# Key roots on ScalarE, the first latent block ahead of the third pair's output, and within-chunk products ahead of the values, in a two-block transformer kernel

## The chip, the cores and the metric

One core of one Trainium2 chip runs the whole program once. The metric is the device time of that execution in microseconds; lower is better.

## What is computed

Two transformer blocks over 512 tokens of width 1024, all in float32. The second block's mixer holds what the change touches: a gated delta rule in chunks (8 heads of width 128, forwards and backwards) beside a latent attention.

```python
qkv = silu(centred_conv(qkv, conv_w))          # 5 taps along the tokens
q, k = l2norm(q), l2norm(k)                    # x * rsqrt(sum(x*x) + 1e-6)
beta = sigmoid(beta_logit); g = -exp(a_log) * softplus(decay_logit + dt_bias)
# per chunk, gc = cumsum(g):
a_mat  = strict_lower((k*beta) @ k.T * exp(gc_i - gc_j))
t_mat  = inverse(eye + a_mat)
u, w   = t_mat @ (v*beta), t_mat @ (k*beta*exp(gc))
qk     = lower(q @ k.T * exp(gc_i - gc_j))
# scan over chunks with state s (128 x 128):
v_new  = u - w @ s
o      = (q*exp(gc)) @ s + qk @ v_new
s      = s*exp(gc_last) + (k*exp(gc_last - gc)).T @ v_new
o_gdn  = rms(o, w_norm) * silu(z)
```

Beside it the latent attention takes 704 columns of the same projection of 512 tokens and 256 context tokens (384 query latents, 256 key and value latents, 64 rotary), normalizes them and goes on from there; 2048 further columns give the gates of the two branches.

## The kernel before

Every large product is made in three products of rounded parts (high by high, high by low, low by high: lines 234, 235 and 237 in `mm3s`). A weight block of 256 columns comes by DMA in two groups of 128 x 1024 values (`weights`). ScalarE makes the high half (line 178) and VectorE the low half (line 179). Raw, high and low tiles share six buffers of one tag. The k, v and q blocks of all pairs are an exception: their halves were made earlier in the program, lie in DRAM as `parts` and come in ready by DMA (line 164). The z, latent and gate blocks are split when they are used.

The gated delta stage (`gdn`) goes over four pairs of heads. Per pair p:

- `inputs`: products for k (512 tokens and 256 context tokens per head), then q (512 tokens). Results land in one of two `pg` banks of PSUM. `conv` copies a result twice on ScalarE, once as it is (line 1254) and once scaled by the middle tap (line 1255), both from PSUM; VectorE adds the four other taps (line 1261), ScalarE applies Silu (line 1263). k is turned by TensorE (line 1291), its squares are summed on ScalarE (line 1316). The sums go to GpSimd, which adds 1e-6 (line 1319), takes the power -1/2 (line 1321) and multiplies to the root (line 1322).
- `values`: products for v like those for k; when v is turned, line 1296 scales it by k's root.
- `betas`: logarithm (line 1351) and reciprocal (line 1353) of the sums, put into the per-token factors `nb` and `bd`.
- `within`: k by k and k by q products (lines 1375, 1377), decays as exponentials on ScalarE (lines 1384 to 1387), masked products on VectorE (lines 1389 to 1391) and the diagonal blocks copied into `X` (lines 1395 and 1397).
- `states`: the inverse of all 32x32 diagonal blocks on VectorE (lines 1405 to 1419, a chain of 62 steps on one engine), block products that complete the inverse (lines 1425 to 1473), and the scan of six steps (lines 1477 to 1542).
- `output`: z products, Silu (line 1550), norm, turn (line 1565) and product with z (line 1567).

The text puts `states(p)` first, then for p+1 `inputs`, `values`, `betas`, `within`, and then `output(p)`. After the last `states` stands `tail()`: the latent products (`mla_latent`, three blocks of 256, 256 and 192 columns, copied to six pages `Z` on line 987) and four blocks of gates (line 863); then the last output.

What sets the order: the SP queue, which issues the loads, keeps the order of the text (`tc.manual_schedule(engines={SP})`). The other engines' instructions are put in an order when the program is built, earlier text first among those that can go; on the chip each engine runs its own list in order. So a later step can fill an engine's gap, but an instruction that waits holds up everything behind it on its engine. Pages of 3 KB (14 of them) hold convolutions, keys, values and `Z`.

Of the kernel before, what the change touches and what calls it, by code (L numbers as in the profile page):

```python
# [75 lines left out]
class Kernel:  # L76
# [766 lines left out]
    def second(self):  # L843
        nc, ap = self.nc, self.ap
# [14 lines left out]
        def gates(j, fs, take, s="a", W=None):  # L859
            for f in fs:  # L860
                for i, ps in self.proj_feat(H, w, 4832 + 1024 * j + f * 256, W=W if f == fs[0] else None):
                    p = self.page([512], s=s)
                    nc.scalar.activation(p, ps, AF.Sigmoid)
                    take(2 * f + i, p)

        def away(j):
            return lambda i, p: nc.scalar.dma_start(GD[j, i], p)

        def tail():
            self.latent = self.mla_latent(H, HC, w)  # L870
            gates(0, range(4), away(0))

        OD = self.gdn(H, HC, w, tail)
        self.wlo_eng = nc.vector
        self.psum(**BANKS_C)
        self.phase(**PHASE_C)
# [92 lines left out]

    def mla_latent(self, H, HC, w):  # L970

        nc, ap = self.nc, self.ap
        act, dve = nc.scalar.activation, nc.vector
        con = self.hb
# [7 lines left out]
        for f0, fn in ((0, 256), (256, 256), (512, 192)):  # L982
            W = self.weights(w, 0, 8, 4128 + f0, fn)
            for X, n, o in ((H, 4, 2), (HC, 2, 0)):
                for t2, ps in self.proj_tok(X, None, 0, n, fn, W):
                    for i in range(2):
                        act(Z[o + 2 * t2 + i][:, f0:f0 + fn], ps[:, i], AF.Copy)
        kr = con.tile([128, 6, 64], F32, name="kr")
        ssr = con.tile([128, 6], F32, name="ssr")
        CQ = [con.tile([128, 2, 512], F32R, name="cq", tag=f"inv{k}") for k in range(3)]  # L990
# [28 lines left out]
        for i in range(2):  # L1019
            nc.scalar.dma_start(gq[64 * i:64 * i + 64], bass.AP(tensor=nm.tensor, offset=nm.offset + 128, ap=[[1, 64], [1, 1]]))  # L1020
        nc.gpsimd.tensor_scalar(ropq, ropq, gq, None, op0=OP.mult)
        return [[c[:, 0], c[:, 1]] for c in CQ], CKV, kr, ssr, ropq, gq

    def mla(self, first, CQ, CKV, kr, ssr, ropq, gqr):

# [210 lines left out]
        g["rows"] = rg  # L1236
        yield g

    def gdn(self, H, HC, w, tail):
        nc, ap = self.nc, self.ap  # L1240
        mm, act, dve = nc.tensor.matmul, nc.scalar.activation, nc.vector
        con = self.const
# [2 lines left out]
        tm = [con.tile([128, 136], F32, name=f"invt{v}") for v in range(2)]  # L1245
        nc.gpsimd.memset(X, 0.0)

        def conv(ps, tile):

            raw, acc = (self.page([sum(p.shape[1] for p in ps)]) for _ in range(2))  # L1250
            o = 0
            for p in reversed(ps):
                n = p.shape[1]
                act(raw[:, o:o + n], p, AF.Copy)
                act(acc[:, o:o + n], p, AF.Copy, scale=cw[:, 48 + tile:49 + tile])  # L1255
                for i in (0, 1, 3, 4):
# [43 lines left out]
        def inputs(pair):  # L1300


            h0 = 2 * pair
            qT, sq_, kT, ktok = ([] for _ in range(4))
            fk = fv = None
            if pair == 0:
                fv = None, ahead(2048)[1]
                fk = ahead(1024)
            kc = [conv(ps, 8 + h0 + f) for f, ps in enumerate(feat(1024 + pair * 256, True, fk))]
            n2, root = [], []  # L1310
            for f, (c, raw) in enumerate(kc):
                kt = self.page([6, 128])
                turn(c, kt)
                ss = self.tmp.tile([128, 6], F32, name="kss")
                for t in range(6):
                    act(raw[:, t * 128:t * 128 + 128], kt[:, t], AF.Square, accum_out=ss[:, t:t + 1])
                n2.append(self.hb.tile([128, 6], F32, name=f"kn2{f}", bufs=2))
                root.append(self.hb.tile([128, 6], F32, name=f"krt{f}", bufs=2))
                nc.gpsimd.tensor_scalar(n2[f], ss, 1e-6, None, op0=OP.add)
                r = self.hb.tile([128, 6], F32, name="krs", bufs=2)  # L1320
                nc.gpsimd.tensor_tensor(r, n2[f], self.mhalf[:, :6], op=OP.pow)
                nc.gpsimd.tensor_tensor(root[f], r, n2[f], op=OP.mult)
                kT.append(c.rearrange("p (a b) -> p a b", a=6))
                ktok.append(kt)
            qc = [conv(ps, h0 + f) for f, ps in enumerate(feat(pair * 256, False))]
            for q, sq in qc:
                qT.append(q)
                act(sq, q, AF.Square)
                pq = self.bank([128, 4], "pt")
                for t in range(4):  # L1330
                    mm(pq[:, t:t + 1], sq[:, t * 128:t * 128 + 128], ones, start=True, stop=True)
                s1 = self.tmp.tile([128, 4], F32, name="qss")
                dve.tensor_copy(s1, pq)
                sq_.append(self.rstd(s1, 1.0 / 128, 128e-6, "qrs"))
            return (qT, kT, ktok), (root, sq_), n2, fv

        def values(pair, root, fv):

            vtok = []
            for f, ps in enumerate(feat(2048 + pair * 256, True, fv)):  # L1340
                c, _ = conv(ps, 16 + 2 * pair + f)
                vt = self.page([6, 128])
                turn(c, vt, root[f])
                vtok.append(vt)
            return vtok

        def betas(pair, n2):
            h0, nb, bd = 2 * pair, [], []
            for f in range(2):
                ln = self.hb.tile([128, 6], F32, name="kln", bufs=2)  # L1350
                act(ln, n2[f], AF.Ln)
                inv = self.hb.tile([128, 6], F32, name="kin", bufs=2)
                dve.reciprocal(inv, n2[f])
                for out, nm, v, op in ((nb, "nb", ln, OP.subtract), (bd, "bd", inv, OP.mult)):
                    out.append(self.hb.tile([128, 6, 2], F32, name=f"k{nm}{f}", bufs=2))
                    dve.tensor_tensor(out[f], g[nm][:, :, h0 + f::8], v[:, :, None].to_broadcast([128, 6, 2]), op=op)
            return nb, bd

        D2 = range(2)
# [219 lines left out]
        for pair in range(4):  # L1579
            O = states(pair, *keys, vtok, bd, *EM)  # L1580
            sq_ = rest[1]
            if pair < 3:
                keys, rest, n2, fv = inputs(pair + 1)
                vtok = values(pair + 1, rest[0], fv)
                nb, bd = betas(pair + 1, n2)
                EM = within(pair + 1, *keys[:2], nb)
            else:
                tail()
            output(pair, O, sq_)
        return OD  # L1590

# [52 lines left out]
```

## Time and profile before

| what | value |
|---|---|
| median of 3 runs | 2276.74 us (2273.09 to 2277.0) |
| the profiled execution | 2269.84 us, span 2268.0 us |
| PE (TensorE) busy | 2166.3 us, 96% |
| DVE (VectorE) busy | 1186.8 us, 52% |
| ACT (ScalarE) busy | 1019.6 us, 45% |
| POOL (GpSimd) busy | 257.4 us, 11% |
| mean granted TensorE clock | 0.986 |

PE is the matrix engine and PEld its weight loads. A row in order of time gives start and duration in microseconds, engine, line, operation, output and inputs by the program's names, shape and count; square brackets hold the idle time of that engine before it and what ended it. The granted clock is 1.00 at 2.4 GHz and 0.50 at 1.2 GHz.

### The profile page before, as it was taken

The numbers are of one execution on the slowest core, as the hardware profiler recorded it, in microseconds if no ns is written. First come the engines' busy times: TensorE is split into PE (matmuls) and PEld (weight loads), VectorE is DVE, ScalarE is ACT, GpSimd is POOL, SyncE is SP. The second block draws the span as 40 slices with busy tenths as digits, with TensorE's granted clock in tenths as the row PEclk, the third lists the DMA queues.
The fourth block names the chain that finished last, engine by engine and source line by source line (L and its number), as shares of the span: only waits on it lengthen the run. The fifth ranks groups of instructions, "written<-read, shape, count | busy, mean of one in ns | idle before, by whom it ended". The sixth has DMA issues, their size and how long they took to land. (4 is left out here: it accounts for less than half of the span.)

```text
span 2268.0 us, 38197 instructions
## 1 busy us (share of the span) xinstructions
PE 2166.3 (96%) x15367; PEld 1921.6 (85%) x15367; DVE 1186.8 (52%) x2636; ACT 1019.6 (45%) x2072; POOL 257.4 (11%) x411
## 2 busy tenths in 40 slices
PE   7999999999999999988999998999999998999999
PEld 7889988788889889867787888789998797898988
DVE  3654453656443233658687775337775444434343
ACT  4542243545443232666666664446564224314231
POOL 0221000001000001203121211201110011020102
PEclk9999999999999999999999998999999999999999
DMA  5233476555772332521222110331013442323232
GB/s 171 74 132 122 159 262 212 173 189 187 248 254 88 98 107 89 183 75 53 75 67 89 53 61 13 97 116 37 30 38 110 169 140 73 99 90 102 94 93 103
DMA packets 195816, 262.05 MB, mean 116 GB/s; under 512 B 12343, under 2 KB 157495, under 8 KB 195639
## 3 DMA queue, kind: packets, MB, share of 16 engines
q1 hardware_dynamic: 188864, 244.61, 33.3%
q10 hardware_dynamic: 6775, 15.00, 1.8%
q8 instruction: 121, 1.98, 0.3%
q14 instruction: 56, 0.46, 0.1%
HBM read 223.39 MB, written 36.18 MB: 114 GB/s over the span
## 5 line engine op out<-in xcount | busy, mean ns | idle before, releaser
L179 DVE TENSOR_TENSOR wlo<-wraw,whi 128x1024 fp32r<-128x1024 f32 (+2 forms) x267 | 321.7, 1205 | 413.6 <-PE pg L235 204.8
L178 ACT ACTIVATE whi<-wraw 128x1024 fp32r<-128x1024 f32 (+2 forms) x267 | 277.0, 1037 | 445.1 <-DMA wraw<-in_w_mlp_out 104.5
L234 PE MATMUL pg<-xhi,whi 128*128 128x512 f32 (+1 forms) x1104 | 428.8, 391 | 25.3 <-ACT a L1255 15.9
L235 PE MATMUL pg<-xlo,whi 128*128 128x512 f32 (+1 forms) x1104 | 425.0, 387 | 0.0
L237 PE MATMUL pg<-xhi,wlo 128*128 128x512 f32 (+1 forms) x1104 | 293.5, 385 | 2.3 <-DVE wlo L179 2.3
L234 PEld LDWEIGHTS pg<-xhi,whi 128*128 128x128 f32 x1104 | 210.6, 191 | 72.5 <-ACT a L1255 18.1
L235 PEld LDWEIGHTS pg<-xlo,whi 128*128 128x128 f32 x1104 | 210.5, 191 | 37.0
L237 PEld LDWEIGHTS pg<-xhi,wlo 128*128 128x128 f32 x1104 | 202.9, 190 | 41.3 <-DVE wlo L179 3.0
L234 PE MATMUL pg<-whi,xhi 128*128 128x256 f32 (+1 forms) x608 | 160.3, 293 | 3.5 <-ACT whi L178 2.6
L235 PE MATMUL pg<-whi,xlo 128*128 128x256 f32 (+1 forms) x608 | 156.5, 288 | 0.0
L234 PE MATMUL sc<-whi,a 128*128 128x256 f32 x560 | 138.2, 281 | 1.6 <-ACT whi L178 1.6
L234 PE MATMUL pg<-whi,a 128*128 128x256 f32 x560 | 138.1, 281 | 0.5 <-DVE a L148 0.5
L235 PE MATMUL sc<-whi,a 128*128 128x256 f32 x560 | 138.4, 281 | 0.0
L235 PE MATMUL pg<-whi,a 128*128 128x256 f32 x560 | 138.0, 280 | 0.0
L234 PEld LDWEIGHTS pg<-whi,xhi 128*128 128x128 f32 x608 | 118.2, 194 | 10.6 <-ACT whi L178 5.2
L235 PEld LDWEIGHTS pg<-whi,xlo 128*128 128x128 f32 x608 | 117.9, 194 | 0.7 <-issue 0.4
L1261 DVE SCALAR_TENSOR_TENSOR a<-a,convw,a 128x511 f32<-128x511 f32 (+3 forms) x160 | 98.2, 642 | 20.1 <-ACT a L1255 19.2
L234 PEld LDWEIGHTS sc<-whi,a 128*128 128x128 f32 x560 | 105.6, 189 | 2.0 <-ACT whi L178 1.8
L237 PE MATMUL pg<-wlo,xhi 128*128 128x256 f32 (+1 forms) x608 | 101.5, 288 | 5.7 <-DVE wlo L179 5.7
L936 POOL TENSOR_TENSOR a<-a,a 128x256 f32<-128x256 f32 x64 | 48.8, 763 | 511.2 <-DVE a L935 510.5
L234 PEld LDWEIGHTS pg<-whi,a 128*128 128x128 f32 x560 | 105.6, 189 | 0.9 <-DVE a L148 0.9
L235 PEld LDWEIGHTS sc<-whi,a 128*128 128x128 f32 x560 | 106.0, 189 | 0.2
(477 smaller groups left out, 4543.1 us busy)
## 6 DMA issues: line engine op xcount, KB each, us to landing
wraw<-in_w_in SPq DMA_DIRECT2D x56, 512.0 KB
fraw<-in_w_mod SPq DMA_DIRECT2D x48, 512.0 KB
parts<-fraw SPq DMA_DIRECT2D x48, 512.0 KB
wraw<-in_w_gate_up SPq DMA_DIRECT2D x44, 512.0 KB
wraw<-in_w_mlp_in SPq DMA_DIRECT2D x32, 512.0 KB
wraw<-in_w_mlp_out SPq DMA_DIRECT2D x32, 512.0 KB
whi<-parts SPq DMA_DIRECT2D x26, 512.0 KB
wlo<-parts SPq DMA_DIRECT2D x26, 512.0 KB
```

The source lines that it names most:

```text
L178: nc.scalar.activation(hi, raw, AF.Copy)
L179: self.wlo_eng.tensor_tensor(lo, raw, hi.bitcast(F32), op=OP.subtract)
L234: mm(out, A[k][0], B[k][0], start=start and k == 0, stop=False)
L235: mm(out, A[k][late], B[k][1 - late], start=False, stop=False)
L237: mm(out, A[k][1 - late], B[k][late], start=False, stop=stop and k == n - 1)
L936: nc.gpsimd.tensor_tensor(self.x[t][:, cs], self.x[t][:, cs], u, op=OP.add)
L1261: dve.scalar_tensor_tensor(y, v, wi, y, op0=OP.mult, op1=OP.add)
```

## The change

Three things. First, the root of k's norm and its logarithm come from ScalarE: one Ln over both heads' sums with 1e-6 as its bias, and one Exp of half of that; VectorE adds 1e-6 for the reciprocal. GpSimd's three instructions per head are gone. With it, `conv` makes its second, scaled copy from the first copy in SBUF and no longer from PSUM. Second, the tail becomes a generator in two pieces: the first block of latents is issued after the third pair's states and before the third pair's output, the rest after the last states. Third, for pairs 1 to 3 `betas` and `within` stand ahead of `values`; for pair 0 the order stays.

```diff
-        def tail():
-            self.latent = self.mla_latent(H, HC, w)
+        def beside():
+            yield from self.mla_latent(H, HC, w)
             gates(0, range(4), away(0))
+            yield
...
                         act(Z[o + 2 * t2 + i][:, f0:f0 + fn], ps[:, i], AF.Copy)
+            if f0 == 0:
+                yield
...
+        eps = con.tile([128, 1], F32, name="keps")
+        nc.gpsimd.memset(eps, 1e-6)
...
                 act(raw[:, o:o + n], p, AF.Copy)
-                act(acc[:, o:o + n], p, AF.Copy, scale=cw[:, 48 + tile:49 + tile])
+                act(acc[:, o:o + n], raw[:, o:o + n], AF.Copy, scale=cw[:, 48 + tile:49 + tile])
...
-                    act(raw[:, t * 128:t * 128 + 128], kt[:, t], AF.Square, accum_out=ss[:, t:t + 1])
-                n2.append(self.hb.tile([128, 6], F32, name=f"kn2{f}", bufs=2))
-                root.append(self.hb.tile([128, 6], F32, name=f"krt{f}", bufs=2))
-                nc.gpsimd.tensor_scalar(n2[f], ss, 1e-6, None, op0=OP.add)
-                r = self.hb.tile([128, 6], F32, name="krs", bufs=2)
-                nc.gpsimd.tensor_tensor(r, n2[f], self.mhalf[:, :6], op=OP.pow)
-                nc.gpsimd.tensor_tensor(root[f], r, n2[f], op=OP.mult)
+                    act(raw[:, t * 128:t * 128 + 128], kt[:, t], AF.Square, accum_out=ss[:, f, t:t + 1])
...
+            ln = self.hb.tile([128, 2, 6], F32, name="kln", bufs=2)
+            act(ln, ss, AF.Ln, bias=eps)
+            root = self.hb.tile([128, 2, 6], F32, name="krt", bufs=2)
+            act(root, ln, AF.Exp, scale=0.5)
...
+            inv = self.hb.tile([128, 2, 6], F32, name="kin", bufs=2)
+            dve.tensor_scalar(inv, ss, 1e-6, None, op0=OP.add)
+            dve.reciprocal(inv, inv)
             for f in range(2):
-                ln = self.hb.tile([128, 6], F32, name="kln", bufs=2)
-                act(ln, n2[f], AF.Ln)
-                inv = self.hb.tile([128, 6], F32, name="kin", bufs=2)
-                dve.reciprocal(inv, n2[f])
...
                 keys, rest, n2, fv = inputs(pair + 1)
-                vtok = values(pair + 1, rest[0], fv)
                 nb, bd = betas(pair + 1, n2)
                 EM = within(pair + 1, *keys[:2], nb)
-            else:
-                tail()
+                vtok = values(pair + 1, rest[0], fv)
+            if pair > 1:
+                next(beside)
             output(pair, O, sq_)
```

## Rows read from the trace of the kernel before

**Rows 1.** The page: busy time of each engine, share of the span.

```profile
PE 2166.3 (96%) x15367; PEld 1921.6 (85%) x15367; DVE 1186.8 (52%) x2636; ACT 1019.6 (45%) x2072; POOL 257.4 (11%) x411
```

**Rows 2.** Stretch: us; PE, PEld, DVE, ACT, POOL busy; PE clock; DMA share; GB/s.

```profile
1016.00:1048.00 32.00, 24.14 (x119) 19.87 (x118) 32.00 (x137) 12.81 (x32) 14.10 (x7) 0.89 0.36 116
...
1058.50:1089.00 30.50, 30.07 (x233) 27.91 (x234) 21.34 (x60) 23.75 (x72) 5.00 (x9) 1.00 0.00 1
1089.00:1123.00 34.00, 31.63 (x170) 24.38 (x169) 19.83 (x41) 27.45 (x71) 6.72 (x7) 1.00 0.36 116
1123.00:1152.00 29.00, 25.22 (x133) 20.70 (x131) 28.97 (x133) 6.97 (x16) 1.41 (x5) 0.99 0.42 133
...
1233.00:1261.00 28.00, 23.12 (x125) 19.52 (x124) 27.97 (x131) 6.37 (x14) 1.10 (x4) 0.99 0.42 140
...
1342.00:1370.00 28.00, 20.00 (x147) 18.96 (x146) 27.93 (x127) 4.46 (x9) 1.22 (x4) 0.87 0.13 37
1370.00:1381.00 11.00, 9.76 (x338) 9.49 (x339) 4.47 (x10) 10.31 (x27) 2.35 (x5) 0.54 0.01 3
...
sum 575.00, PE 528.26 PEld 452.20 DVE 377.38 ACT 346.45 POOL 101.29; mean PE 31.07 PEld 26.60 DVE 22.20 ACT 20.38 POOL 5.96
```

**Rows 3.** PE's waits, 930 to 1515 us: total, times, longest.

```profile
PE pg L234 <- ACT a L1255: 15.9, 8, 6.8
PE pg L237 <- DVE wlo L179: 7.5, 3, 4.0
PE sc L1433 <- DVE inv L1418: 7.0, 3, 3.2
```

**Rows 4.** Line 1319: shortest, median and longest duration in ns.

```profile
L1319 POOL TENSOR_SCALAR kn<-kss x8: 247/496/11157, 950.6 to 1281.2; 128x6 f32<-128x6 f32 x8
```

**Rows 5.** Order of time in the first inverse.

```profile
1026.03 11.16 POOL L1319 TENSOR_SCALAR kn<-kss 128x6 f32<-128x6 f32 x1 [52.54 <-ACT a L1316]
1026.11 0.39 PE L234 MATMUL pg<-xhi,whi 128*128 128x512 f32 x1
...
1028.83 0.39 PE L234 MATMUL pg<-xhi,whi 128*128 128x512 f32 x1
...
1037.22 0.21 ACT L1351 ACTIVATE kln<-kn 128x6 f32<-128x6 f32 x1 [9.98 <-POOL kn L1319]
...
1038.54 0.79 PE L234 MATMUL pg<-xhi,whi 128*128 128x512 f32 x1 [6.83 <-ACT a L1255]
...
1043.04 0.39 PE L234 MATMUL pg<-xhi,whi 128*128 128x512 f32 x1
```

**Rows 6.** Order of time on ACT after the second pair's scan.

```profile
1203.08 0.84 ACT L1263 ACTIVATE a<-a 128x768 f32<-128x768 f32 x1 [3.96 <-DVE a L1261]
...
1208.05 1.28 ACT L1387 ACT_TABLE_LOAD   x1
1209.35 1.15 ACT L1387 ACTIVATE w<-sc,knb 128x128 f32<-128x128 f32 x4
```

**Rows 7.** Order of time between two k products, second pair.

```profile
1134.01 0.60 ACT L1254 ACTIVATE a<-pg 128x512 f32<-128x512 f32 x1 [5.25 <-PE pg L237]
...
1137.69 0.50 PE L234 MATMUL pg<-xhi,whi 128*128 128x512 f32 x1 [0.84 <-ACT a L1255]
```

**Rows 8.** Order of time on PE, first pair's values.

```profile
989.74 0.79 PE L234 MATMUL pg<-xhi,whi 128*128 128x512 f32 x1 [4.31 <-ACT a L1255]
```

**Rows 9.** ACT by line, 1123 to 1233 us: count | busy us, mean ns | idle before.

```profile
L1387 ACT ACTIVATE w<-sc,knb 128x128 f32<-128x128 f32 x16 | 4.7, 368 | 2.0 <-PE sc L1385 2.0
L1395 ACT ACTIVATE inv<-w 32x192 f32<-32x192 f32 x8 | 2.9, 357 | 0.1
```

**Rows 10.** DVE's groups by line, 1016 to 1342 us.

```profile
L1261 DVE SCALAR_TENSOR_TENSOR a<-a,convw,a 128x510 f32<-128x510 f32 (+3 forms) x115 | 71.0, 647 | 1.4 <-ACT a L1255 1.0
```

**Rows 11.** Order of time in the last inverse.

```profile
1345.04 0.74 PE L237 MATMUL pg<-wlo,xhi 128*128 128x256 f32 x4 [1.75 <-DVE wlo L179]
...
1365.46 1.38 PE L237 MATMUL pg<-wlo,xhi 128*128 128x256 f32 x8 [3.99 <-DVE wlo L179]
```

More of the change, by code (lines that the diff above doesn't have):

```diff
@@ L867, in away @@
             return lambda i, p: nc.scalar.dma_start(GD[j, i], p)
-        def tail():
-            self.latent = self.mla_latent(H, HC, w)
+        def beside():
+            yield from self.mla_latent(H, HC, w)
             gates(0, range(4), away(0))
-        OD = self.gdn(H, HC, w, tail)
+            yield
+        OD = self.gdn(H, HC, w, beside())
         self.wlo_eng = nc.vector
@@ L1021, in mla_latent @@
         nc.gpsimd.tensor_scalar(ropq, ropq, gq, None, op0=OP.mult)
-        return [[c[:, 0], c[:, 1]] for c in CQ], CKV, kr, ssr, ropq, gq
+        self.latent = [[c[:, 0], c[:, 1]] for c in CQ], CKV, kr, ssr, ropq, gq
     def mla(self, first, CQ, CKV, kr, ssr, ropq, gqr):
@@ L1237, in gdn_gates, with gdn @@
         yield g
-    def gdn(self, H, HC, w, tail):
+    def gdn(self, H, HC, w, beside):
         nc, ap = self.nc, self.ap
@@ L1309, in inputs @@
             kc = [conv(ps, 8 + h0 + f) for f, ps in enumerate(feat(1024 + pair * 256, True, fk))]
-            n2, root = [], []
+            ss = self.hb.tile([128, 2, 6], F32, name="kss", bufs=2)
             for f, (c, raw) in enumerate(kc):
@@ L1313, in inputs @@
                 turn(c, kt)
-                ss = self.tmp.tile([128, 6], F32, name="kss")
                 for t in range(6):
-                    act(raw[:, t * 128:t * 128 + 128], kt[:, t], AF.Square, accum_out=ss[:, t:t + 1])
-                n2.append(self.hb.tile([128, 6], F32, name=f"kn2{f}", bufs=2))
-                root.append(self.hb.tile([128, 6], F32, name=f"krt{f}", bufs=2))
-                nc.gpsimd.tensor_scalar(n2[f], ss, 1e-6, None, op0=OP.add)
-                r = self.hb.tile([128, 6], F32, name="krs", bufs=2)
-                nc.gpsimd.tensor_tensor(r, n2[f], self.mhalf[:, :6], op=OP.pow)
-                nc.gpsimd.tensor_tensor(root[f], r, n2[f], op=OP.mult)
+                    act(raw[:, t * 128:t * 128 + 128], kt[:, t], AF.Square, accum_out=ss[:, f, t:t + 1])
                 kT.append(c.rearrange("p (a b) -> p a b", a=6))
                 ktok.append(kt)
+            ln = self.hb.tile([128, 2, 6], F32, name="kln", bufs=2)
+            act(ln, ss, AF.Ln, bias=eps)
+            root = self.hb.tile([128, 2, 6], F32, name="krt", bufs=2)
+            act(root, ln, AF.Exp, scale=0.5)
             qc = [conv(ps, h0 + f) for f, ps in enumerate(feat(pair * 256, False))]
@@ L1334, in inputs @@
                 sq_.append(self.rstd(s1, 1.0 / 128, 128e-6, "qrs"))
-            return (qT, kT, ktok), (root, sq_), n2, fv
+            return (qT, kT, ktok), (root, sq_), (ss, ln), fv
         def values(pair, root, fv):
@@ L1342, in values @@
                 vt = self.page([6, 128])
-                turn(c, vt, root[f])
+                turn(c, vt, root[:, f])
                 vtok.append(vt)
@@ L1348, in betas @@
             h0, nb, bd = 2 * pair, [], []
+            ss, ln = n2
+            inv = self.hb.tile([128, 2, 6], F32, name="kin", bufs=2)
+            dve.tensor_scalar(inv, ss, 1e-6, None, op0=OP.add)
+            dve.reciprocal(inv, inv)
             for f in range(2):
-                ln = self.hb.tile([128, 6], F32, name="kln", bufs=2)
-                act(ln, n2[f], AF.Ln)
-                inv = self.hb.tile([128, 6], F32, name="kin", bufs=2)
-                dve.reciprocal(inv, n2[f])
                 for out, nm, v, op in ((nb, "nb", ln, OP.subtract), (bd, "bd", inv, OP.mult)):
                     out.append(self.hb.tile([128, 6, 2], F32, name=f"k{nm}{f}", bufs=2))
-                    dve.tensor_tensor(out[f], g[nm][:, :, h0 + f::8], v[:, :, None].to_broadcast([128, 6, 2]), op=op)
+                    dve.tensor_tensor(out[f], g[nm][:, :, h0 + f::8], v[:, f, :, None].to_broadcast([128, 6, 2]), op=op)
             return nb, bd
```

## The prediction

> **What bounds the kernel now.** I read the page first, then busy time by stretch, then who held TensorE up, then the instructions in order of time at the longest holds. The page says that PE is busy 96% of a span of 2268.0 us [rows 1], so a change that removes no PE work can only win where PE stands, or runs at its lower clock. The change touches the gated delta stretch, about 935 to 1510 us. There PE is busy 528 of 575 us (the sum of [rows 2]), so 47 us stand open. Two thirds of them have three named holders: `ACT a L1255` 15.9 us in 8 holds, `DVE wlo L179` 7.5, `DVE inv L1418` 7.0 [rows 3].
>
> By stage, a pair of heads goes round in 107 us (inverse begun at 1016, the next at 1123): the inverse, DVE's alone (28 to 32 us, DVE busy all of it), a chain of small block products (10.5 us, between the rows that end at 1048 and begin at 1058.5), the scan (30.5 us, PE full), then outputs and the next pair's within part (34 us). Open PE time lies in the inverses: 32.0 - 24.1 = 7.9, 29.0 - 25.2 = 3.8, 28.0 - 23.1 = 4.9 and 28.0 - 20.0 = 8.0 us, together 24.6 [rows 2]. There PE lives on what was made ready before DVE went into the inverse. In the first and the last of these the granted clock falls to 0.89 and 0.87, and in the block products after the last to 0.54: a mixture of 2.4 and 1.2 GHz, after PE stood. The scan shows 1.00 and nothing to win.
>
> **The change part by part.** The sum is made against the profiled execution, 2269.84 us (span 2268.0 and 1.84 around it). The median of the three runs is 2276.74, that is 6.90 above it; I add that at the end.
>
> (a) *Roots off POOL.* Per pair two adds, two powers and two products leave POOL; one Ln and one Exp of 128x12 on ACT and one add on DVE come. On seven of eight occasions the POOL add took well under 2 us, but the one that fell inside the first inverse took 11.16 us against a median of 0.50 [rows 4]. ACT had loaded its table for the Ln and stood 9.98 us behind that add; behind the Ln were queued the two copies that free TensorE's pg banks, and PE stood 6.83 us [rows 5]. In the new order the Ln reads sums that ACT itself made, so this wait cannot recur. After the hold the clock is lower: the first twelve 512-column matmuls take 4.50 us (1038.54 to 1043.04), twelve ahead of it 2.72 (1026.11 to 1028.83), so 0.227 each. That costs 1.8 us [rows 5]. What takes the place of the wait: the third pair of products (values), whose weights need no split: 2 x (24 x 0.227 + 24 x 0.114) = 16.4 us of PE work, more than the hole (a product of 256 columns at half of one of 512). Worth 6.8 + 1.8 = **8.6 us**. Not below zero: the removed wait had no other use.
> Table loads: Ln has two per pair, 1.28 us each, like all [rows 6]; one Ln for both heads leaves one, and possibly one for the Exp, which the trace doesn't price. So 0 to 1 load saved, plus a Silu reload between the two Ln: on ACT 1.3 to 2.6 us per pair, mostly beside PE work. I take **1 us** for all pairs, with 0 to 4 as bounds.
>
> The load's price first by the row: 1.28 us, and the activation behind it starts 0.02 us later (1208.05, 1209.35 [rows 6]). The Trainium skill (ScalarE: Activation LUTs, What ACT_TABLE_LOAD costs) gives about 2.66 us per switch with a drain. By that rule, a separate load for the Exp in each of four pairs would add 10.6 us to ACT, by the row 5.1. No row here shows the drain, so the sum goes by the row.
>
> (b) *Second conv copy from SBUF.* A pg bank is now held until L1255 has read it; then it is free after L1254. At 1134.01 ACT had copied the 512-column bank, but L1255 waited for the 256-column product to end; PE stood 0.84 us until one of the two L1255 was done [rows 7]. Free after L1254, that bank is open 3 us earlier and the hold vanishes. Of the 15.9 us [rows 3] 6.83 are counted above; 4.31 at 989.74 belong to the first pair, where ACT was late with both copies [rows 8], so I leave them. The remaining six holds are 15.9 - 6.8 - 4.3 = **4.8 us**. The bound below is 0, if ACT puts the copy itself later. The second copy itself stays one ACT instruction over the same columns.
>
> (c) *Within part ahead of values.* Within needs 12 x 2 exponentials at 0.37 us (8.9 us of ACT) and 8 small copies at 0.36 (2.9) [rows 9], yet the stretch from scan to inverse is 34 us [rows 2]. It is stretched because values go first: in the second pair ACT stands 3.96 us for DVE's convolution before a Silu at 1203.08, and the first exponential comes only at 1209.35, behind that Silu and another table load [rows 6]. Moved ahead, the inverse can start some 10 us earlier, with up to 16.4 us of values' products left to feed PE in it. This is no PE work saved: its worth is open PE time in the inverses not already counted. Of the 24.6 us, 6.8 are (a), about 4.4 are (b) (all but one of the six holds), and 5.7 in the last go to (d); 7.7 remain. Half is in reach, since PE's queue is in order and three times stood in front of a product that needs `inv` itself, 7.0 us in all [rows 3]: **3.5 us**, bounds 0 to 7.7. DVE's convolutions of the values (16 x 0.647 = 10.4 us per pair [rows 10]) now come after within and before the inverse in emission order. They fit into DVE's open time there (34 - 19.8 = 14.2 us [rows 2]).
>
> (d) *First latent block ahead of the third pair's output.* In the last inverse PE lives on latent blocks whose low halves DVE must still make: PE stands 1.75 and 3.99 us for L179 [rows 11], and 11 us at clock 0.54 follow [rows 2]. Now the first block's split is done before, and with values (c) also left over there are 16.4 + 16.4 us of PE work (144 products of 256 columns at 0.114) for an inverse of 28 us. That removes 5.7 us and perhaps a third of the low-clock stretch's 0.46 x 11 = 5.1 us, 1.7: **7.4 us**, bounds 0 to 13. What moves along: on SP the small loads of `rotg` and `ropx` and two weight loads now stand ahead of the two z weight loads of the third pair; z products come later by one block, behind PE work that is there anyway. The block's six Z pages of 3 KB must come free first; 14 less the 6 of keys and values and 4 of the running convolutions leaves 4 until these end.
>
> (e) *New friction.* Nothing in the trace shows the new order on ACT, where exponentials that wait for PE now precede the copies that free pg. The nearest rows: holds of the kind seen, 0.8 us each, up to one like 4.31 us per pair [rows 7, 8]. I take **-4 us** for three pairs; the bounds are 0 and -13.
>
> Sum: 8.6 + 1 + 4.8 + 3.5 + 7.4 - 4 = 21 us. 2269.84 - 21 = 2249; with 6.90, **2256 us** as median.
>
> **The rivals.**
> *Handed on (2271).* PE has the same work per turn; values' products pulled into the hole at 1031 are then missing as filler in the scan and around the block products, and the z weights, which need free weight buffers and DVE, come no earlier. For: the hole is one of 47 us, spread thin. Against: the scans are full now (30.1 of 30.5 us [rows 2]), so what leaves them is room for z. Then only (b) and 1 us of (a) stay, 5.8 us: 2271.
> *All inverses full (2239).* Everything at its upper bound: 8.6 + 4 + 4.8 + 7.7 + 13 - 0 = 38 us. For: DVE and ACT have room. Against: static order against real times, as at 1365.
> *Slower (2286).* On ACT the exponentials stand ahead of the values' copies. If values' products are not done when the scan ends, both pg banks stay full while ACT waits for the within chain, PE has nothing but within's own 8 us, and the stretch that now has PE busy 31.6 of 34 us dries up. It decides from about 7 us per pair: 3 x 7 = 21 eats the gain. At 10 us per pair the result is 2256 + 30 = 2286. For: both banks are ACT's to free, and the 4.31 us hold is of this kind. Against: with (b) copies need one instruction per bank, and values' products start in the scan already.
> *It doesn't do what it says (2276).* If Ln and Exp cost two loads and the engines' order comes out as before, (a)'s hole is merely displaced into another wait for ACT: no change.
>
> **How the numbers follow.** Forecast (2246 to 2268): 0.52. All full (2232 to 2246): 0.12. Handed on (2267 to 2275): 0.16, half of it beyond 0.2%. No effect (2273 to 2280): 0.06. Slower (2279 to 2300): 0.14. 0.2%, 4.6 us, is about what a measurement of this kernel can tell from no change. Faster: 0.52 + 0.12 + 0.08 = 0.72; same 0.08 + 0.06 = 0.14; slower 0.14. The range leaves out a third of "all full" and most of "slower": 2237 to 2279.
>
> **What would show it.** (a) No L1319 row, no ACT idle of 10 us in the first inverse, values' products there instead. (b) `ACT a L1255` nearly gone from TensorE's waits. (c) The first exponential within 3 us of the scan's end, the next inverse earlier by about 10 us. (d) No wait for L179 in the last inverse, clock above 0.54 after it. Wrong would be: PE waits of over 2 us for ACT's first conv copy while ACT waits for PE's score products; a turn of 107 us as before in spite of an earlier inverse (handed on); or a scan that gets longer than 33 us.

## The result, and the profile after

The changed kernel takes **2300.03 us** (median of 4 runs, 2297.53 to 2302.53) against 2276.87 for the kernel before in the same comparison: 23 us more, ratio 1.011 (95% interval 1.0097 to 1.0122). 2256 was forecast, with 2237 to 2279 as range. The profiled execution took 2300.94 us (span 2299.1 and 1.84 around it), close to its median; that of before lay 7.0 us under its own.

PE still bounds it. Its busy time went up by 20.5 us [rows 1] with the same 15367 instructions:

```profile
PE 2186.8 (95%) x15367; PEld 1941.8 (84%) x15367; DVE 1188.3 (52%) x2636; ACT 1010.8 (44%) x2063; POOL 226.6 (10%) x388
```

The stretches that answer to [rows 2] (same columns). The inverses begin at 1028.3, 1127, 1237 and 1354.4; the last row is the whole gated delta stretch, 591 us where it was 575:

```profile
1028.30:1060.60 32.30, 21.98 (x121) 18.74 (x119) 32.30 (x138) 11.58 (x30) 1.34 (x4) 0.87 0.35 115
1060.60:1071.10 10.50, 9.82 (x336) 8.85 (x336) 8.53 (x16) 9.66 (x26) 4.70 (x10) 0.58 0.02 5
1071.10:1105.10 34.00, 32.74 (x239) 29.59 (x236) 21.29 (x62) 26.60 (x76) 1.95 (x5) 0.95 0.01 1
1105.10:1127.00 21.90, 17.48 (x104) 13.68 (x102) 17.23 (x39) 15.34 (x54) 6.71 (x8) 1.00 0.08 25
1127.00:1159.00 32.00, 29.98 (x157) 24.72 (x160) 31.72 (x137) 9.64 (x22) 1.39 (x5) 0.95 0.51 156
...
1196.00:1237.00 41.00, 37.79 (x197) 30.49 (x196) 23.83 (x50) 25.12 (x65) 6.47 (x9) 0.92 0.16 49
1237.00:1271.50 34.50, 28.89 (x138) 23.40 (x138) 33.39 (x138) 13.78 (x32) 1.35 (x4) 0.90 0.34 111
...
1308.00:1354.40 46.40, 42.37 (x229) 34.99 (x228) 28.86 (x64) 33.58 (x100) 5.55 (x9) 0.96 0.21 63
1354.40:1388.40 34.00, 31.02 (x200) 28.54 (x201) 33.93 (x137) 14.26 (x34) 1.35 (x4) 0.90 0.17 49
1388.40:1403.00 14.60, 10.83 (x354) 9.81 (x352) 6.70 (x13) 9.76 (x24) 1.37 (x4) 0.77 0.32 104
...
935.00:1526.00 591.00, 534.63 (x4367) 460.35 (x4368) 384.58 (x1126) 340.40 (x907) 71.08 (x131) 0.94 0.23 72
```

PE's waits in the same part of the program (930 to 1540 us), against [rows 3]:

```profile
PE sc L1437 <- DVE inv L1422: 11.7, 3, 9.0
PE pt L1298 <- ACT a L1270: 7.8, 3, 3.7
PE pg L234 <- ACT a L1261: 6.7, 3, 3.2
PE pg L237 <- DVE wlo L179: 4.3, 1, 4.3
```

ScalarE's second copy (then L1255, 15.9 us) is gone as a holder; in its place stand the inverse itself (L1422 is L1418 of before), the values' Silu (L1270) and the first copy (L1261). The low clock has spread: 0.92, 0.90 and 0.96 in stretches that had 1.00 or 0.99 before (1193 to 1233, 1233 to 1261 and 1305 to 1342).

PE's own list divides the time in another way. Between the starts of its 6001st and its 10401st record, which bracket what the change touches, lie 561.4 us before and 577.7 after: **16.3 more in the stretch**. The profiles differ by a further 9.3 us ahead of it and 5.4 behind it, where the code is the same. Some of that is the fast profile of before. The rest is not chance, as the experiments show: nearly all products of 256 weight columns against a page as the stationary side came 2.8 ns further apart (mean 117.16 ns before, 119.96 after, about 3335 of them: 9.3 us), all over the program, at full clock. Only 168 of them stand in the stretch.

### The profile page after: what moved, and what is told of

It reads as the page before. It is cut to its first block, busy times and chain, and to the rows that moved or that the text cites. A ratio compares the mean times of both kernels' runs of the same rounds, so it can differ in the third digit from the quotient of the medians.

```text
span 2299.1 us, 38183 instructions
## 1 busy us (share of the span) xinstructions
PE 2186.8 (95%) x15367; PEld 1941.8 (84%) x15367; DVE 1188.3 (52%) x2636; ACT 1010.8 (44%) x2063; POOL 226.6 (10%) x388
## 5 line engine op out<-in xcount | busy, mean ns | idle before, releaser
L179 DVE TENSOR_TENSOR wlo<-wraw,whi 128x1024 fp32r<-128x1024 f32 (+2 forms) x267 | 321.3, 1204 | 424.7 <-PE pg L235 214.7
L234 PE MATMUL sc<-whi,a 128*128 128x256 f32 x560 | 140.8, 283 | 1.6 <-ACT whi L178 1.6
L234 PE MATMUL pg<-whi,a 128*128 128x256 f32 x560 | 141.0, 284 | 0.5 <-DVE a L148 0.5
L235 PE MATMUL sc<-whi,a 128*128 128x256 f32 x560 | 141.1, 284 | 0.0
L235 PE MATMUL pg<-whi,a 128*128 128x256 f32 x560 | 140.8, 283 | 0.0
L234 PEld LDWEIGHTS pg<-whi,a 128*128 128x128 f32 x560 | 107.5, 192 | 1.0 <-DVE a L148 0.9
L235 PEld LDWEIGHTS pg<-whi,a 128*128 128x128 f32 x560 | 107.6, 192 | 0.0
L1268 DVE SCALAR_TENSOR_TENSOR a<-a,convw,a 128x510 f32<-128x510 f32 (+3 forms) x160 | 98.1, 640 | 16.7 <-ACT a L1262 15.3
```

Source lines behind the costliest of these rows:

```text
L179: self.wlo_eng.tensor_tensor(lo, raw, hi.bitcast(F32), op=OP.subtract)
L234: mm(out, A[k][0], B[k][0], start=start and k == 0, stop=False)
L235: mm(out, A[k][late], B[k][1 - late], start=False, stop=False)
```

## The experiments

Each is timed against the kernel before on the chip that it ran on; the medians of before lie within 2.5 us of each other. "Stretch" is the time between those two records in the profile, "product" the mean spacing of the products just named.

| run | what | median us | ratio (95%) | stretch us | product ns |
|---|---|---|---|---|---|
| before | | 2274.4 to 2276.9 | | 561.4 | 117.2 |
| after | all parts | 2300.0 | 1.0097 to 1.0122 | 577.7 | 120.0 |
| e1 | roots alone | 2310.2 | 1.0126 to 1.0168 | 592.3 | 120.0 |
| e2 | conv copy alone | 2273.7 | 0.9987 to 1.0011 | 559.6 | 116.6 |
| e3 | within alone | 2288.9 | 1.0034 to 1.0062 | 577.5 | 117.2 |
| e4 | latent block alone | 2277.9 | 0.9998 to 1.0020 | 565.1 | 116.7 |
| e5 | after, values first | 2290.3 | 1.0042 to 1.0082 | 569.1 | 120.0 |
| e6 | after, old roots | 2282.2 | 1.0016 to 1.0041 | 570.1 | 116.7 |
| e7 | before, latent halves made early | 2290.7 | 1.0041 to 1.0083 | 557.7 | 116.2 |
| e8 | e1, latent halves made early | 2310.0 | 1.0127 to 1.0177 | 566.6 | 120.0 |
| e9 | before + 64 bytes | 2283.5 | 1.0021 to 1.0047 | 564.0 | 119.7 |
| e10 | after + 64 bytes | 2287.8 | 1.0037 to 1.0064 | 579.7 | 116.7 |
| e11 | e1 + 64 bytes | 2295.1 | 1.0070 to 1.0109 | 584.4 | 116.7 |
| e12 | e10, inverse ahead of values | 2342.0 | 1.0273 to 1.0306 | 621.2 | 117.2 |
| e13 | e11, root on GpSimd | 2294.4 | 1.0049 to 1.0093 | 583.2 | 116.7 |
| e14 | e10, values first | 2281.5 | 1.0014 to 1.0047 | 568.6 | 117.0 |
| e15 | before + 2 x 64 bytes | 2276.9 | 0.9990 to 1.0014 | 562.3 | 117.8 |
| e16 | before, x moved | 2272.9 | 0.9980 to 1.0003 | 561.2 | 115.9 |

### One part at a time (e1 to e4)

Each takes its own hunks of the diff and leaves the others out. **e1**, roots:

```diff
-                nc.gpsimd.tensor_scalar(n2[f], ss, 1e-6, None, op0=OP.add)
...
-                nc.gpsimd.tensor_tensor(r, n2[f], self.mhalf[:, :6], op=OP.pow)
...
+            act(ln, ss, AF.Ln, bias=eps)
...
+            act(root, ln, AF.Exp, scale=0.5)
```

> The kernel before with the change of the key roots alone (Ln and Exp on ScalarE, no GpSimd). The forecast's theory: the 6.83 us hold in the first inverse goes and values' products take its place, -8.6 us, and one table load less, -1: together about -10 us, and TensorE waits for `inv` in the first inverse under 2 us. The rival (handed on): what TensorE can do in an inverse is bounded by the 3 KB pages into which its results are copied, so values' products can't come earlier; the hole comes back at the inverse's end as a wait of 5 to 9 us for `inv`: 0 us, within 3.

Measured: +35 us, outside both. Its trace shows three separate things: the longer products (9.4 us over the program), and two places in the stretch. Together they make some 26 of the 35 us; the rest was not traced. The first place is the last inverse, 1364.7 to 1393. The rows in order of time:

```profile
1363.23 1.06 ACT L178 ACTIVATE whi<-wraw 128x1024 fp32r<-128x1024 f32 x1
...
1366.59 1.18 DVE L179 TENSOR_TENSOR wlo<-wraw,whi 128x1024 fp32r<-128x1024 f32 x1
...
1386.91 1.22 DVE L179 TENSOR_TENSOR wlo<-wraw,whi 128x1024 fp32r<-128x1024 f32 x1
...
1388.18 1.22 PE L237 MATMUL pg<-wlo,xhi 128*128 128x256 f32 x4 [14.68 <-DVE wlo L179]
```

A latent block has two groups of weights. Before, the first group's low half was made ahead of the inverse (begun at 1341.9) and the second's just inside:

```profile
1334.34 1.22 DVE L179 TENSOR_TENSOR wlo<-wraw,whi 128x1024 fp32r<-128x1024 f32 x1 [0.53 <-ACT whi L178]
...
1343.81 1.18 DVE L179 TENSOR_TENSOR wlo<-wraw,whi 128x1024 fp32r<-128x1024 f32 x1
```

Here ScalarE made the first high half only 1.5 us ahead of the inverse, so the first low half fell inside it and the second into its end, 20 us later, though its high half was ready at 1366. PE stood 14.68 us (3.99 at the inverse's end before, for the second block [rows 11]). The second place is the scan, where PE waits for ScalarE. Second scan of e1, order of time:

```profile
1190.09 1.28 ACT L1326 ACT_TABLE_LOAD   x1
1191.39 0.30 ACT L1326 ACTIVATE kln<-kss,keps 128x12 f32<-128x12 f32 x1
...
1193.29 1.28 ACT L1328 ACT_TABLE_LOAD   x1
...
1194.82 1.28 ACT L1270 ACT_TABLE_LOAD   x1
...
1198.48 1.05 PE L1335 MATMUL pt<-ones,a 128*128 128x1 f32 x8 [1.15 <-ACT a L1332]
...
1201.29 0.64 PE L1494 MATMUL sc<-w,a 128*128 128x128 f32 x2
```

Three table loads come within 6 us (before, three in the like scan too, but spread over 10 us). PE stands 1.15 us, and behind it pairs of products take 0.43 us from start to start (0.22 further on in the same scan): the lower clock. That scan took 34.3 us, with the clock at 0.95; before, 30.7 at 1.00 (the first three scans together 99.9 and 93.7). Before, then e1, columns as in [rows 2]:

```profile
1162.20:1192.90 30.70, 30.70 (x243) 29.03 (x244) 21.95 (x63) 25.73 (x82) 6.99 (x11) 1.00 0.00 1
```

```profile
1178.70:1213.00 34.30, 33.15 (x249) 31.12 (x247) 23.17 (x65) 26.96 (x83) 2.57 (x5) 0.95 0.01 1
```

**e2**, conv copy:

```diff
-                act(acc[:, o:o + n], p, AF.Copy, scale=cw[:, 48 + tile:49 + tile])
+                act(acc[:, o:o + n], raw[:, o:o + n], AF.Copy, scale=cw[:, 48 + tile:49 + tile])
```

> The kernel before with the second conv copy read from SBUF alone. The forecast's theory: the six small holds for ScalarE's second copy vanish, -4.8 us. The rival: they vanish, but TensorE then reaches the end of its work in each inverse as much earlier and waits for `inv` that much longer: 0 us, within 2.

Measured: no change; the rival. PE's waits, 930 to 1515 us (L1259 is the first copy, L1423 the end of the inverse):

```profile
PE sc L1438 <- DVE inv L1423: 10.3, 4, 3.0
PE pg L237 <- DVE wlo L179: 8.1, 3, 2.8
PE pg L234 <- ACT a L1259: 7.1, 2, 4.1
```

The holds for ScalarE's copies fell from 15.9 us to 7.1, and the wait for `inv` grew from 7.0 to 10.3. The other 5.5 us do not show in the time.

**e3**, within:

```diff
-                vtok = values(pair + 1, rest[0], fv)
                 nb, bd = betas(pair + 1, n2)
                 EM = within(pair + 1, *keys[:2], nb)
+                vtok = values(pair + 1, rest[0], fv)
```

> The kernel before with only each pair's betas and within part ahead of its values (pairs 1 to 3). The forecast's theory: the inverse starts earlier with values' products as work in it, -3.5 us (0 to -7.7). The rival, from the trace of the changed kernel: VectorE's taps of the values come behind within's masked products and fall into the inverse, which gets 3 to 6 us longer (28.6 us before); ScalarE's Silu waits for them, and behind it TensorE's turn of the values and the copies that free its pg banks: 3.5 + 1.7 us of TensorE waits in each of the last two inverses: +10 to +18 us in all.

Measured: +14 us, within the rival's 10 to 18. The inverses of the second to fourth pair took 30.3, 38.6 and 36.4 us (28.4 to 28.6 before), and one wait for a low half in the last inverse took 8.7 us (two, of 5.7 us together, before).

**e4**, latent block:

```diff
-            else:
-                tail()
+            if pair > 1:
+                next(beside)
```

> The kernel before with only the first latent block ahead of the third pair's output. The forecast's theory: no wait for the low halves in the last inverse and less of the low clock behind it, -7.4 us (0 to -13). The rival: the block's work is taken from the stretch behind the last inverse or the pages hold it back, so that only the two waits for the low half move: -2 us, within 2. If this part costs something by itself, the z products that it is put ahead of come too late for the third pair's output: +2 to +6 us.

Measured: +3 us, not told from none. The waits for low halves grew (7.5 us before) instead of going:

```profile
PE pg L234 <- ACT a L1260: 16.0, 8, 6.8
PE pg L237 <- DVE wlo L179: 12.7, 4, 9.8
```

With the first block done earlier, it is the second block's low half that comes late in the same inverse.

### Two parts less, and low halves out of the way (e5 to e8)

**e5** and **e6** undo one part of the changed kernel: e5 the hunk shown under e3, e6 that under e1.

> The changed kernel with values ahead of betas and within again: roots, conv copy and latent block together. If the parts' costs simply add (roots +35, conv 0, latent +2): 2312 us. If most of the roots' loss is one place, TensorE's 14.7 us wait for a low half that VectorE makes in the middle of the last inverse, then the latent block put ahead moves that place too: 2290 to 2300 us, with a wait for the low half under 6 us in the last inverse.

> The changed kernel with the key roots on GpSimd again: conv copy, within part and latent block together. If the parts' costs add (conv 0, within +13, latent +2): 2290 us. By the forecast's own prices (the roots gain 9.6) it would be slower than the changed kernel: 2310 us. If the roots cost in the scans what their trace shows there (some 3 us a scan, from the loads of Ln's and Exp's tables): 2285 to 2292 us.

e5 came at 2290.3, so the parts don't add: the roots' 35 and the latent block's 2 give 15 together. Its wait for a low half was not under 6 us, though: 8.6, where e1 had 14.68. e6 came at 2282.2, below all three of its figures. No wait for a low half is left in its last inverse, as in the changed kernel; with the within part taken out instead (e5) it is there.

**e7** and **e8** add the first two latent blocks to those whose halves are made earlier in the program:

```diff
-                blocks = [f + 256 * pair for pair in range(4) for f in (1024, 2048, 0)]
+                blocks = [f + 256 * pair for pair in range(4) for f in (1024, 2048, 0)] + [4128, 4384]
```

> The kernel before, and beside it the halves of the first two latent blocks made earlier in the program and laid down in DRAM like those of k, v and q, so that no low half for them is made in the last inverse. The forecast's step (d), by another road: TensorE's waits for low halves in the last inverse (5.7 us) and part of the low clock behind it go, -5 to -7 us, less 0 to 4 us for the earlier work: 2268 to 2275 us. The rival (pages and banks bound what TensorE does in an inverse): the wait moves to `inv`, 0 to +4 us.

> Roots by ScalarE alone, with the same latent halves made earlier. If the place of the low half in the last inverse makes 11 to 16 us of the roots' 35: 16 to 24 us above the run of the kernel before with the same halves made earlier. If the loss lies in ScalarE's table loads in the scans and in the first pair alone: still 30 to 37 us above it.

e7 missed both numbers, because the earlier work was mispriced (0 to 4 us): the 6001st record comes at 920.2 us instead of 893.3. In the stretch it gains 3.7 us, and in its last inverse no wait for L179 is left. For e8 the 19.3 us above e7 hit the first theory. By stretch: roots cost 592.3 - 561.4 = 30.9 us with the low halves made in place (23.0 with e11's placement) and 566.6 - 557.7 = 8.9 with them out of the way; by the times, 35.2 and 19.3. So 14 to 22 us of the roots' loss hang on where VectorE makes the latent weights' low halves.

### Placement (e9 to e11, e15, e16)

The new roots need a constant `keps` (4 bytes, which take 32) and give up the 64 bytes of the old sums. By the program's layout the weight tiles move from byte 25472 to 25504 of a partition and the pages from 89024 to 88992: counted in lines of 128 bytes, 64 bytes apart before, level after. (That 128 bytes are a unit of the chip is a guess that no run settles.) **e9** to **e11** put 64 unused bytes (32, in two buffers) ahead of the pages:

```diff
+        pad = self.tmp.tile([128, 8], F32, name="kpad")
+        nc.gpsimd.memset(pad, 0.0)
```

> The kernel before with one more small tile (64 bytes of each partition, cleared once and used by nothing) ahead of the pages. PE, ScalarE, VectorE and SyncE have the same instructions in the same order; only the pages lie 64 bytes further on, so that a page and a weight tile begin at the same place of a 128-byte line, as in the kernels with the new roots; in the kernel before they begin 64 bytes apart. Theory of the placement: the 3346 products of 256 weight columns with a page as the stationary side go from a median of 118 to 120 ns (117.2 to 120.0 in the mean), and the time by +8 to +11 us. Rival (an effect of the roots' own instructions): 118 ns and 0 us, within 3.

> The changed kernel with the same small tile, which takes pages and weights 64 bytes apart again. Theory of the placement: those products at 118 ns again, -8 to -11 us: about 2290, and what is left (13 us above the kernel before) is the order of the work. Rival: 120 ns, 2300.

> Roots by ScalarE alone with the small tile. Theory of the placement: 2310 - 10 = 2300, and the 25 us left are in the stretch: 11 in the last inverse (a low half), some 7 in the three scans, some 6 between them. Rival: 2310.

Forty microseconds of the last large product in before, after, e9 and e10, each from its own answer (columns as in [rows 2]; the count after PE's busy time is what to read):

```profile
2115.40:2155.40 40.00, 40.00 (x342) 40.00 (x341) 13.18 (x18) 7.92 (x8) 7.35 (x10) 1.00 0.29 93
```

```profile
2144.60:2184.60 40.00, 40.00 (x335) 40.00 (x335) 12.79 (x17) 7.28 (x8) 7.17 (x10) 1.00 0.29 93
```

```profile
2127.00:2167.00 40.00, 40.00 (x336) 40.00 (x335) 12.43 (x17) 7.42 (x7) 6.61 (x9) 1.00 0.29 93
```

```profile
2136.00:2176.00 40.00, 40.00 (x342) 40.00 (x341) 12.64 (x17) 7.42 (x7) 6.62 (x9) 1.00 0.29 95
```

PE is never idle and at full clock in all four; 342 products fit where pages and weights lie 64 bytes apart, 335 or 336 where they don't. e9, with PE's, ScalarE's, VectorE's and SyncE's instructions unchanged, loses 8.8 us by that alone (beside it there is only a GpSimd memset at the program's start), e10 wins 12.3 against the changed kernel and e11 15.2 against e1, both more than expected (8 to 11, and 10). A fourth pair, e5 against e14 below, differs by the pad alone as well: 8.9 us. So **9 to 12 of the 23 us are placement**, shown by adding it to the old kernel and by taking it from the new; each figure is known to 2 to 4 us, by the scatter of its runs. The spacing does not explain all of e11's gain: 8 of its 15 us lie in the stretch, where few of these products stand.

**e15** moves x (the large input tiles) against the weights as well, **e16** only where x is the stationary side (the edit is that of e16, whose tiles are 128 bytes longer and begin 16 values, 64 bytes, further on in the first block):

```diff
-        XT = self.xT_tiles()
+        XT = self.xT_tiles(16 if i == 0 else 0)
```

> The kernel before with 64 unused bytes ahead of the two large x tiles and 64 ahead of the pages: pages and weights stay 64 bytes apart, x and weights, which begin at the same place of a 128-byte line in all kernels so far, stand 64 apart too. Same instructions in the same order. If what counts is how the two operands of a product stand to each other: the 1827 products of 256 weight columns with x as the stationary side go from 120 to 118 ns (-4 us), and those of 512 x columns with weights as the stationary side (2931, 227 ns) move too, by a price not known: -4 to +6 us. If only the pages' own place counts: 120 and 227 ns as before, 0 us within 2.

> The kernel before, with the x tiles of the first projections and of the first output product alone begun 64 bytes further on (their last 128 bytes are added to the tile, so all other tiles keep their place in a line). These are the stages in which x is the stationary side of 256 weight columns, up to 390 us; where x is the 512-column moving side it stays where it was. Theory of the two operands' distance: some 1730 products go from 120 to 114 ns as in e15, the others stay: -8 to -10 us, 2265 to 2267. Rival (what e15 won came from elsewhere and its loss too): 0 us, within 2.

e15: the products with x stationary went from a median of 120 to 114 ns, those with 512 x columns moving from 227 to 229; the time did not move. e16: 114 ns again, as its theory said, but 227 became 228 with the high x tile, which had not moved, and 233 with the low one, which had moved by 128 bytes. The time, 1.5 us less, is not told from none, as its rival said. The products against a page changed too, though pages and weights still stand 64 bytes apart and the pages had moved by 256 bytes: 114.7 ns behind the stretch, where before had 117.8. So the place of both operands counts, by 2 to 6 ns a product, but "64 bytes apart in a line of 128" is not the whole rule. What the rule is stays open.

### What is left without the placement (e12 to e14)

**e12** is e10 with the inverse issued ahead of the pair's values (`next(S)` goes up to the end of the inverse):

```diff
-                vtok = values(pair + 1, rest[0], fv)
+                vtok = []
+                S = states(pair + 1, *keys, vtok, bd, *EM)
+                next(S)
+                vtok += values(pair + 1, rest[0], fv)
```

> The changed kernel with the small tile, and each pair's inverse issued ahead of its values, so that VectorE puts no taps of the values into it. If the longer inverses (34 us against 28.6) and what waits for them are most of what the within part costs: inverses of 29 to 30 us again and 5 to 10 us less than with the small tile alone. If the loss is the thin stretch before the inverse and TensorE's wait for the values' Silu, these get longer as the inverse gets shorter, since the taps come after it: 0 to +8 us.

Measured: +54 us against e10, outside both. The second pair's inverse:

```profile
1144.44 1.21 DVE L179 TENSOR_TENSOR wlo<-wraw,whi 128x1024 fp32r<-128x1024 f32 x1
...
1145.71 1.22 PE L237 MATMUL pg<-xhi,wlo 128*128 128x512 f32 x2 [25.65 <-DVE wlo L179]
```

Now the z weights' low half stands at the end of the inverse in VectorE's list, and PE stands 25.65 us. The inverses did get shorter (30.6, 32.2 and 32.2 us; 31.8, 34.0 and 34.1 in e10), but PE's waits for low halves came to 44.9 us: what an inverse gained by being alone, PE paid for what VectorE owed it.

**e13** is e11 with the logarithm left on ScalarE and the root given back to GpSimd (the edit below). **e14** is e10 with values ahead of within (the hunk shown under e3, undone).

```diff
-            act(root, ln, AF.Exp, scale=0.5)
...
+            nc.gpsimd.tensor_scalar(n2, ss, 1e-6, None, op0=OP.add)
...
+                nc.gpsimd.tensor_tensor(r, n2[:, f], self.mhalf[:, :6], op=OP.pow)
+                nc.gpsimd.tensor_tensor(root[:, f], r, n2[:, f], op=OP.mult)
```

> The kernel before with only the logarithm taken from the sums by ScalarE (one Ln for both heads, 1e-6 as its bias); the root stays on GpSimd, so there is no Exp for it. Small tile as in e11, so that pages and weights stand 64 bytes apart. If the scans' loss with the new roots (some 4 us in three scans at 64 bytes) comes from two table loads in a row ahead of the scan's copies: that goes, and 2288 to 2292 us is left of 2295. If it comes from the order that one Ln for both heads forces on the last inverse (a wait of 13.5 us for a low half): 2290 to 2296 us with this wait still there; if any change of the order moves this wait: 2274 to 2282.

> Roots, conv copy and latent block together, values ahead of within, with the small tile. Theory of the placement: 2290 - 10 = 2280 us, and so the within part costs 7 to 8 us of the 13 that the changed kernel with the small tile stands above the kernel before. Rival (within costs nothing once the latent block is ahead): 2286 to 2290 us.

e13: 2294.4, as its second case said. The second scan in e11, then in e13, which has no load for the Exp:

```profile
1167.60:1200.30 32.70, 31.55 (x248) 29.58 (x247) 22.65 (x64) 26.89 (x83) 2.56 (x5) 1.00 0.00 1
```

```profile
1165.60:1197.10 31.50, 31.50 (x249) 29.58 (x246) 22.44 (x63) 25.23 (x81) 6.17 (x10) 1.00 0.00 1
```

So the load does cost about a microsecond a scan (the first and third scan give 1.3 and 1.0 us). But the 14.2 us wait for a low half stands, and the total is the same. e14: 2281.5, as the placement said. So within costs 2287.8 - 2281.5 = 6.3 us in the company of the other parts, and the three others together 2281.5 - 2274.8 = 6.7; both are known to some 3 to 4 us. Roots in that company, with the placement taken out, cost 2287.8 - 2282.2 = 5.6 us (e10 against e6), where alone they cost 20 (e11). The conv copy and the latent block were not taken out of e10 one by one.

No version tried is clearly faster than the kernel before. The account of the 23 us: 9 to 12 placement, about 6 the within part, about 7 roots, conv copy and latent block together in the order that they force.

## Why the prediction was wrong, step by step

**Bound: right. Places: half right.** PE bounds both kernels, and half of its open time before was in the inverses (24.6 of 47 us). What the change opened lies around them too: 4.4, 3.2 and 4.0 us in the stretches between a scan and the next inverse (2.4, 0.7 and 1.5 before).

**(a) Roots: the wait went, the gain did not come.** No row of L1319 is left, and the Ln waits for GpSimd no more. The step that failed is the one under "What takes the place of the wait": that the products of the values would fill the hole. PE went on without that hold and was done with all that stood ahead of L1437 in its list by 1049.9; then:

```profile
1049.25 0.63 PE L237 MATMUL pg<-hc,wlo 128*128 128x256 f32 x4
1058.82 1.48 ACT L1448 ACTIVATE w<-inv 32x192 f32<-32x192 f32 x4 [11.72 <-DVE inv L1422]
1058.93 0.39 PE L1437 MATMUL sc<-inv,w 32*32 32x32 f32 x4 [9.05 <-DVE inv L1422]
...
1081.79 0.85 ACT L1261 ACTIVATE a<-pg 128x256 f32<-128x256 f32 x2
```

Both pg banks were full. Their copies stood behind L1448 in ScalarE's list, which waited 11.72 us for the inverse, and came at 1081.79; the next product into pg starts at 1083.43. The hole of 6.83 us became one of 9.05, PE was busy 22.0 of 32.3 us in the first inverse (24.1 of 32.0 before), and the clock in the block products behind it was 0.58 (0.83 before, from 1048.1 to 1058.4). That it would be the 3 KB pages that hold PE back, as e1's rival said, is not so: by the layout the two pages for those copies had last been used at 1006 and 1009. The table loads, priced at 1 us gained, had the wrong sign where the roots stand alone: e1 has 53 of them in the program, before 49, and the Exp's cost about a microsecond a scan (e13). The changed kernel has 40, nine fewer than before, and its time shows no gain from them. On the price of one, the Trainium skill (ScalarE: Activation LUTs, What ACT_TABLE_LOAD costs) has a drain of about 1.38 us beside it; here again there is none, 1190.09 and 1.28 and the next activation at 1191.39.

**(b) Conv copy: at its lower bound.** 0 was named, 4.8 taken. The holds went and were handed on to the end of the inverse (e2).

**(c) Within: half right.** The first turn did shrink, from 107.4 to 98.3 us between inverses, the "10 us earlier" of the text, and its first exponential came before the scan's end. The next two turns did not: 109.9 and 117.5 us (109.6 and 109.0 before), with the first exponential 14 and 22 us behind the scan's end (16 and 14 before), though within stands ahead of values in the text. The step that failed is that the values' taps "fit into DVE's open time there". They fall into the inverse, and from the second pair on it took 31.9, 34.6 and 34.1 us (28.4 to 28.6 before). In the third:

```profile
1237.05 1.28 ACT L1270 ACT_TABLE_LOAD   x1 [6.07 <-DVE a L1268]
...
1239.24 0.87 PE L1298 MATMUL pt<-ident,a 128*128 128x128 f32 x6 [3.47 <-ACT a L1270]
...
1242.01 0.80 PE L234 MATMUL pg<-xhi,whi 128*128 128x512 f32 x1 [1.89 <-ACT a L1261]
...
1244.59 3.25 DVE L1268 SCALAR_TENSOR_TENSOR a<-a,convw,a 128x255 f32<-128x255 f32 x6
...
1256.78 1.41 DVE L1571 SCALAR_TENSOR_TENSOR a<-pt,onw,a 128x512 f32<-128x512 f32 x2 [1.07 <-PE pt L1569]
```

Taps (L1268) and even the output's product (L1571, which waits for PE in the middle of the inverse) stand between the steps of a chain of 62. ScalarE's Silu waits for the taps that VectorE ends just ahead of the inverse, PE's turn of the values waits for the Silu (3.47), and the copy that frees pg comes behind both (1.89). The rival called slower named ScalarE's exponentials ahead of the values' copies; the holder was the Silu behind VectorE. It is the same trade, one engine further on. Forecast 3.5 us gained, measured 6.3 lost, give or take 4 (e10 against e14).

**(d) Latent block: right in its place, wrong in sum.** In the changed kernel the last inverse has no wait for L179, and PE is busy 31.0 of 34.0 us there (20.0 of 28.0 before). That takes the latent block and the within part together: without within the wait is 8.6 us (e5, e14). Nor was the block's split "done before": its second low half was made at 1363.8, inside the inverse. The stretch ahead of the inverse grew from 37 to 46.4 us, and the block products behind it took 14.6 us at 0.77, with a 3.8 us hold (11 at 0.54 before). Alone it is worth nothing (e4), since the next low half is late instead.

**(e) Friction: mis-sized, and with another holder.** 4 us were taken, 13 the bound, for exponentials ahead of the copies that free pg. In the last two inverses PE stood 3.47 and 3.75 us for the values' Silu, which waited for taps, and 1.89 and 1.59 for the copies behind it; the longest wait for a first copy, 3.2 us, was in the first pair, where the order is the old one. The stretch as a whole lost 16.3 us, so the friction was larger than all gains. Of the signs of being wrong one came plainly: a scan longer than 33 us, the first, with 34.0 at a clock of 0.95.

**What was not in the sum at all** is placement, 9 to 12 us: the rows of before show no product at two addresses. With it taken out (2288), the time still lies outside the range. That it is near the *slower* rival's 2286, to which 0.14 was given, is luck: the holder was another.

The common error is one of view. Holes were priced one by one, as if what fills a hole were free to move there. Each engine runs a list that was made when the program was built; a change in one place made other lists for all engines, and whatever small instruction, a low half or a tap, falls into the 28 us in which VectorE is taken comes late or makes the chain longer. PE's longest wait for a low half in the last inverse ranges from none (after, e6) to 14.7 us (e1).

## What to carry to other kernels

Where one engine is taken for a long chain, price a change by what the other engines will be owed during that chain, and look in the lists for what falls into it, before counting holes. A hole that ends because one engine's wait is removed comes back at the next in-order wait, unless work and a free buffer for its result are both at hand. When a change adds or drops a tile, compare the spacing of untouched products too: a few nanoseconds on thousands of them can outweigh the change.

## What the runs showed of the hardware

- The spacing of back-to-back products depends on where their operands lie. For 3335 products of 256 columns the mean was 119.7 to 120.0 ns in the five profiles with pages and weights level, and 115.9 to 117.8 in the thirteen with 64 bytes between them; e9 differs from before by a 64-byte pad alone. With x as the stationary side 120 or 114 ns, with 512 moving columns of x 227 to 233 (e15, e16).
- In e1, PE stood 1.15 us in a scan until 1198.48; the granted clock was 0.50 from 1200.8 to 1204.2 (pairs of products 0.43 us apart instead of 0.22) and 1.00 on either side.
